# Seven block products in place of eight for the FFN input product of a decoder step

## The chip, the cores and the metric

The kernel runs on one core of a Trainium2 chip. Its engines are TensorE (PE, with its weight loads as PEld), VectorE (DVE), ScalarE (ACT), GpSimd (POOL) and SyncE (SP), each of which works through a queue of its own in order. The time is device microseconds for one execution, the median over runs; the profile is one execution more, with a time of its own.

## The reference: what is computed

One layer of a hybrid decoder (retention, gated MLP with spatial mixing, merge, FFN) over 512 prompt tokens and 8 sample tokens, so 520 columns in all, with width 1024. The part that matters here is the FFN:

```
D_FF = ((8 * D_MODEL // 3 + 255) // 256) * 256        # 2816
...
hn = rms_norm(h, norm_ffn_g)
f_gate, f_up = jnp.split(hn @ w_ffn_in, 2, axis=-1)
h = h + ((jax.nn.silu(f_gate) * f_up) @ w_ffn_down).astype(x.dtype)
...
y = rms_norm(h, norm_final_g)
```

All of it is float32. `w_ffn_in` is 1024 x 5632, `w_ffn_down` 2816 x 1024.

## The kernel before

Activations lie transposed: 128 features on the partitions, the 520 tokens along the free dimension, in two halves of 260 (`HT`). TensorE multiplies in a reduced form of float32 (fp32r), so each operand is split in two: `hi` is the value rounded to fp32r, `lo` is what is left. `split` makes `hi` on ACT and `lo` on DVE. A product of two operands is then three matmuls, hi x hi, hi x lo and lo x hi.

`weights` loads one tile of 128 x 1024 weights by SP (`wraw`, three buffers) and splits it into `whi` and `wlo` (two buffers each). `product` issues the matmuls of one 128 x 128 piece: three terms by two token halves, six matmuls of 128x260. A weight tile with eight such pieces is 48 matmuls into one PSUM tile of two banks (`acc_psum`, two buffers).

The last stages run in this order. `w_o` (tiles `ps_wo`): eight tiles of 48 matmuls; each result plus the residual goes to `hs`, and ACT and DVE make the scaled split `hg` of it. Then the FFN input: for each of 22 tiles of 128 hidden features one tile of the gate (`ps_fg`) and one of the up half (`ps_fu`); DVE multiplies both with `rstd`, ACT takes the silu, POOL multiplies gate and up (`fa`), and `split` makes `act`. Then the FFN output (`ps_fd`): eight tiles of 22 pieces, 132 matmuls each. The last of the eight is done in two token halves of 66 matmuls, so that the final norm of the first half (a sum over features by a matmul with ones, `ps_ss`, then four DVE and ACT operations for the root, then the scaling of all rows and the store) runs beside the matmuls of the second half.

The order on each engine comes from a scheduler that places instructions when the program is built; the pools of buffers bound it. `big` holds 26 pairs of 128 x 2 x 520, and the FFN keeps its `act` tiles there.

The names: `wraw`, `whi`, `wlo` are weights as loaded and split; `hg` and `act` are activations; `ps_...` are PSUM tiles; `fa`, `fb` are gate and up values.

Of the kernel before, what the change touches and what calls it, by code (L numbers as in the profile page):

```python
# [29 lines left out]
NBIG = 26  # L30
NFP = 4
# [10 lines left out]
def step_kernel(ctx: ExitStack, tc: tile.TileContext, io):  # L42
# [41 lines left out]
    def weights(src, n, cuts=(), keep=False):  # L84

        raw = wp.tile([P, 8 * P], F32, name="wraw", tag="wraw", bufs=3)
        if keep:
            hi, lo = flat(wide("khi", F32R)), flat(wide("klo", F32R))
        else:
            hi = wp.tile([P, 8 * P], F32R, name="whi", tag="whi")  # L90
            lo = wp.tile([P, 8 * P], F32R, name="wlo", tag="wlo")
# [448 lines left out]
    def gmlp(gp):  # L540
# [187 lines left out]
    a = None  # L728
    for i in range(NF):
        a, b = ttile("fa"), ttile("fb")  # L730
        pg = ev(ffn_tile(i, "ps_fg"))
        if i == 0:

            nc.scalar.copy(out=halves(a), in_=pg)
            pg = halves(a)
            pu = ev(ffn_tile(NF, "ps_fu"))
            nc.scalar.copy(out=halves(b), in_=pu)
            pu = halves(b)
            row_rstd(rstd, row_sums(sq), D)
            sq = const.tile([P, T], F32, name="sq")  # L740
        nc.vector.tensor_tensor(out=halves(a), in0=pg, in1=halves(rstd), op=ALU.mult)
        nc.scalar.activation(out=a, in_=a, func=AF.Silu)
        if i > 0:
            pu = ev(ffn_tile(NF + i, "ps_fu"))
        nc.vector.tensor_tensor(out=halves(b), in0=pu, in1=halves(rstd), op=ALU.mult)  # L745
        nc.gpsimd.tensor_tensor(out=a, in0=a, in1=b, op=ALU.mult)  # L746
        pr = fp.tile([P, 2, T], F32R, name=f"act{i}") if i < NFP else pair(f"act{i}")
        split(pr[:, 0, :], pr[:, 1, :], a)
        act.append(pr)

    def down_weights(i, keep=False):

        for k0 in range(0, NF, 8):
            n = min(8, NF - k0)
            yield weights(io["w_ffn_down"][i][:, k0 * P : (k0 + n) * P], n, keep=keep), k0, n

    def down(ps, blocks, fs=(0, 1)):
        for w, k0, n in blocks:
            for k in range(k0, k0 + n):
                product(ps, w, k - k0, act[k], k == 0, k == NF - 1, fs)  # L760

    rsqrt_table(a)

    hn = []
    for i in range(KT - 1):
        ps = acc_psum("ps_fd")
        down(ps, down_weights(i))
        hi = hs[:, i, :]
        nc.vector.tensor_tensor(out=halves(hi), in0=ev(ps), in1=halves(hi), op=ALU.add)
        add_square(sq, hi, i == 0)  # L770
        nc.scalar.activation(out=hi, in_=hi, func=AF.Copy, scale=gains[:, 2, i : i + 1])
        hn.append(hi)
# [102 lines left out]
```

## Time and profile before

| what | value |
|---|---|
| median of 3 runs | 1168.37 us (1165.16 to 1168.41) |
| the profiled execution's own time | 1165.98 us |
| its span, first to last instruction | 1164.2 us |
| instructions in the span | 21641 |
| mean granted TensorE clock | 0.990 |
| PE busy | 1142.0 us, 98% of the span |
| DVE busy | 668.8 us, 57% |
| ACT busy | 435.8 us, 37% |
| POOL busy | 209.8 us, 18% |

Busy time of PE counts overlapping matmuls once, and a pipelined matmul's record is longer than what it adds; what one matmul adds is read from a stretch of many. The time outside the span, 1165.98 less 1164.2, is 1.8 us.

### The profile page before, as it was taken

The numbers are of one execution on the slowest core, as the hardware profiler recorded it, in microseconds if no ns is written. First come the engines' busy times: TensorE is split into PE (matmuls) and PEld (weight loads), VectorE is DVE, ScalarE is ACT, GpSimd is POOL, SyncE is SP. The second block draws the span as 40 slices with busy tenths as digits, with TensorE's granted clock in tenths as the row PEclk, the third lists the DMA queues.
The fourth block names the chain that finished last, engine by engine and source line by source line (L and its number), as shares of the span: only waits on it lengthen the run. The fifth ranks groups of instructions, "written<-read, shape, count | busy, mean of one in ns | idle before, by whom it ended". The sixth has DMA issues, their size and how long they took to land.

```text
span 1164.2 us, 21641 instructions
## 1 busy us (share of the span) xinstructions
PE 1142.0 (98%) x9242; PEld 1125.6 (97%) x9242; DVE 668.8 (57%) x1040; ACT 435.8 (37%) x672; POOL 209.8 (18%) x175
## 2 busy tenths in 40 slices
PE   8999999999999999999999999999999999999995
PEld 7999999999999998999999999999999999999995
DVE  7788738885787589538434456445545454532233
ACT  4366345433653365323223432343222232322220
POOL 7213201420141013002111222211101010101101
PEclk9999999999999999999999999999999999999998
DMA  7267336633763284222222223422232222223222
GB/s 266 86 217 286 110 110 237 244 109 117 261 212 127 74 276 162 73 91 74 90 74 73 91 91 117 139 94 92 88 106 81 104 90 93 87 90 97 86 78 74
DMA packets 44928, 147.53 MB, mean 127 GB/s; under 512 B 5360, under 2 KB 7808, under 8 KB 44824
## 3 DMA queue, kind: packets, MB, share of 16 engines
q1 hardware_dynamic: 37152, 118.76, 30.2%
q0 software_dynamic: 7680, 27.38, 6.4%
q8 instruction: 73, 1.20, 0.4%
q14 instruction: 23, 0.19, 0.0%
HBM read 125.02 MB, written 21.10 MB: 126 GB/s over the span
## 4 chain that ended last, share of the span: by engine, by line
PE 84%; DVE 7%; DMA 3%; ACT 3%; issue 2%; POOL 0%; DVEq 0%; ACTq 0%; POOLq 0%; SPq 0%
PE ps_fg L105 11%; PE ps_fu L105 11%; PE ps_fd L105 10%; PE ps_ro L105 8%; PE ps_v L105 6%; PE ps_ar L105 4%; PE ps_gm L105 4%; PE ps_g L105 4%; PE ps_gu L105 4%; PE ps_wo L105 4%; PE ps_gv L105 4%; PE ps_ag L105 3%; PE k L105 3%; PE q L105 2%; PE ps_o L460 1%
## 5 line engine op out<-in xcount | busy, mean ns | idle before, releaser
L79 ACT CAST whi<-wraw 128x1024 fp32r<-128x1024 f32 (+2 forms) x180 | 184.8, 1027 | 484.9 <-issue 96.3
L82 DVE TENSOR_TENSOR wlo<-wraw,whi 128x1024 fp32r<-128x1024 f32 (+2 forms) x180 | 256.4, 1425 | 99.2 <-ACT whi L79 94.4
L105 PE MATMUL ps_fg<-hg,whi 128*128 128x260 f32 x704 | 112.5, 282 | 0.0
L105 PE MATMUL ps_fu<-hg,whi 128*128 128x260 f32 x704 | 112.5, 282 | 0.0
L105 PE MATMUL ps_fd<-act,whi 128*128 128x260 f32 x616 | 98.8, 282 | 0.0
L105 PEld LDWEIGHTS ps_fg<-hg,whi 128*128 128x128 f32 x704 | 96.2, 188 | 0.0
L105 PEld LDWEIGHTS ps_fu<-hg,whi 128*128 128x128 f32 x704 | 96.2, 188 | 0.0
L105 PEld LDWEIGHTS ps_fd<-act,whi 128*128 128x128 f32 x616 | 84.4, 188 | 0.0
L105 PE MATMUL ps_g<-xg,whi 128*128 128x260 f32 x512 | 82.7, 283 | 0.0
L105 PE MATMUL ps_ro<-gated,whi 128*128 128x260 f32 x512 | 82.6, 283 | 0.0
L105 PE MATMUL ps_v<-xg,whi 128*128 128x260 f32 x512 | 82.3, 282 | 0.0
L105 PEld LDWEIGHTS ps_ro<-gated,whi 128*128 128x128 f32 x512 | 70.6, 188 | 0.7 <-issue 0.2
L105 PE MATMUL ps_fu<-hg,wlo 128*128 128x260 f32 x352 | 70.8, 282 | 0.0
L105 PE MATMUL ps_fg<-hg,wlo 128*128 128x260 f32 x352 | 70.8, 282 | 0.0
L105 PEld LDWEIGHTS ps_v<-xg,whi 128*128 128x128 f32 x512 | 70.1, 188 | 0.0
L105 PEld LDWEIGHTS ps_g<-xg,whi 128*128 128x128 f32 x512 | 69.9, 188 | 0.0
L746 POOL TENSOR_TENSOR fa<-fa,fb 128x520 f32<-128x520 f32 x22 | 28.8, 1308 | 227.6 <-ACT whi L79 192.8
L442 ACT ACTIVATE kv<-qkb,vs 128x256 f32<-128x256 f32 x128 | 54.1, 498 | 26.9 <-DMA qkb<-qks 23.9
L105 PE MATMUL ps_fd<-act,wlo 128*128 128x260 f32 x308 | 61.8, 282 | 0.0
L745 DVE TENSOR_TENSOR fb<-ps_fu,rstd 128x520 f32<-128x520 f32 x21 | 14.7, 700 | 75.1 <-PE ps_fu L105 75.1
L163 POOL TENSOR_TENSOR sq<-sq,sqr 128x520 f32<-128x520 f32 x19 | 32.9, 1732 | 132.7 <-ACT sqr L161 128.4
L447 DVE SCALAR_TENSOR_TENSOR junk<-S,qkb 128x256 f32<-128x256 f32 x128 | 54.0, 422 | 2.3
(250 smaller groups left out, 2509.3 us busy)
## 6 DMA issues: line engine op xcount, KB each, us to landing
wraw<-in_w_in SPq DMA_DIRECT2D x78, 512.0 KB, 3.5
wraw<-in_w_ffn_in SPq DMA_DIRECT2D x44, 512.0 KB, 3.5
S<-in_st SPq DMA_DIRECT2D x32, 512.0 KB, 4.4
out_rss<-S POOLq DMA_DIRECT2D x32, 512.0 KB, 4.6
qkb<-qks POOLq DMA_DIRECT2D x16, 512.0 KB, 5.0
wraw<-in_w_ret_o SPq DMA_DIRECT2D x16, 512.0 KB, 3.5
wraw<-in_w_ffn_down SPq DMA_DIRECT2D x16, 512.0 KB, 3.5
wraw<-in_w_gm_o SPq DMA_DIRECT2D x8, 512.0 KB, 3.5
```

The lines of the kernel that those rows point to most:

```text
L79: nc.scalar.copy(out=hi, in_=src)
L82: (lo_eng or nc.vector).tensor_tensor(out=lo, in0=src, in1=hi.bitcast(F32), op=ALU.subtract)
L105: nc.tensor.matmul((ps[f] if isinstance(ps, list) else ps[:, f])[:, 0:HT], a, x[:, k, f * HT : (f + 1) * HT], start=first and n == 0, stop ...
L163: (add or nc.gpsimd).tensor_tensor(out=acc, in0=acc, in1=q, op=ALU.add)
L442: nc.scalar.activation(out=kv[:, j, :], in_=kb, func=AF.Copy, scale=vs[:, j, b : b + 1])
L447: nc.vector.scalar_tensor_tensor(out=junk, in0=S[:, j, :], scalar=1.0, in1=qb, op0=ALU.mult, op1=ALU.mult, accum_out=os_[:, j, b : b + 1],)
L460: nc.tensor.matmul(ps[:, s * P : NP], vtile(s, l)[:, j * P : (j + 1) * P], score(s, k), start=i == 0, stop=i == 11,)
L745: nc.vector.tensor_tensor(out=halves(b), in0=pu, in1=halves(rstd), op=ALU.mult)
L746: nc.gpsimd.tensor_tensor(out=a, in0=a, in1=b, op=ALU.mult)
```

## The change

The FFN input product is regrouped. A block is now two pieces of 128 hidden features (the gate and the up tile of the same number) by two halves of the 1024 input features, against the two token halves: a 2 x 2 by 2 x 2 product of blocks. In place of eight block products there are seven (Strassen's algorithm), each of four pieces by three terms by one half of tokens, 12 matmuls of 128x260 (`seven`, order a, b, s1, s2, s3, s4, d). They accumulate into three PSUM banks, and between products partial sums are copied out or added (`seen`).

The activations' sums are formed once, after `w_o` (`sum_acts`). The weights' sums are formed for each of 22 blocks (`sum_weights`): `s13` by two plain loads and an adding DMA issued by POOL, `s24` by two DVE additions, and the block `d` by a casting DMA into `wdh`, a negated copy on ACT into `wdl`, and an adding DMA into `wdl`. Three pairs of 128 x 1024 are then split as before.

Hidden features are handled in groups of 8, 8 and 6: up to ten blocks of the input product are run, then the output product over a group's pieces, added to `hs` (DVE multiplies with `rstd`, POOL adds); the last group takes the final norm. `rstd` is multiplied in before the silu by POOL, and the up half's factor after the output product. The pools are changed: `big` has 24, tables of the first stages lie in pools that are closed after the heads, and their room holds two more buffers each of `wraw`, `whi` and `wlo` (`wq`) and two of `wdh` and `wdl`.

```
-NBIG = 26
-NFP = 4
+NBIG = 24
+NACT = 10
...
+    wpools = {"wraw": [wp] * 3, "whi": [wp] * 2, "wlo": [wp] * 2}
...
+    first.close()
+    wq = ctx.enter_context(tc.tile_pool(name="wq", bufs=2))
+    for k in wpools:
+        wpools[k] = wpools[k] + [wq] * 2
...
+    ORDER = "a b s1 s2 s3 s4 d".split()
+    MEETS = dict(a=0, s1=1, b=2, d=6, s4=3, s3=4, s2=5)
...
+        s13 = block(wtile("wraw", F32))
+        for i in range(2):
+            nc.sync.dma_start(out=s13[:, i], in_=src[:, 0])
+        nc.gpsimd.dma_start(out=s13, in_=src[:, 1:3], accum_op=ALU.add)
+        ab = block(wtile("wraw", F32))
+        nc.sync.dma_start(out=ab, in_=src[:, 2:4])
+        dh = wq.tile([P, 4 * P], F32R, name="wdh")
+        dl = wq.tile([P, 4 * P], F32R, name="wdl")
+        nc.gpsimd.dma_start(out=dh, in_=src[:, 1])
+        nc.scalar.activation(out=dl, in_=dh.bitcast(F32), func=AF.Copy, scale=-1.0)
+        nc.gpsimd.dma_start(out=dl, in_=src[:, 1], accum_op=ALU.add)
+        s24 = block(wtile("wraw", F32))
+        nc.vector.tensor_tensor(out=s24[:, 0], in0=s13[:, 0], in1=ab[:, 0], op=ALU.add)
+        nc.vector.tensor_tensor(out=s24[:, 1], in0=s24[:, 0], in1=ab[:, 1], op=ALU.add)
+        w = {"d": (dh, dl)}
+        for names, t in (("a b", ab), ("s1 s3", s13), ("s2 s4", s24)):
+            w |= dict(zip(names.split(), both(t.rearrange("p a b -> p (a b)"))))
...
+            tt(out=x[:, 4], in0=x[:, 3], in1=x[:, 1], op=ALU.subtract)
+            tt(out=x[:, 1], in0=x[:, 0], in1=x[:, 1], op=ALU.subtract)
+            stt(out=x[:, 5], in0=x[:, 3], scalar=-1.0, in1=x[:, 1], op0=ALU.mult, op1=ALU.subtract)
+            stt(out=x[:, 6], in0=x[:, 5], scalar=-1.0, in1=x[:, 2], op0=ALU.mult, op1=ALU.subtract)
...
+            split(h, l, x[:, 0:4])
...
+        bank = [ps[:, 0, 0:HT], ps[:, 1, 0:HT], aux(f"{name}3")[:, 0:HT]]
+        into = dict(a=0, b=2, s1=1, s2=0, s3=0, s4=1, d=0)
...
+                for n, (ww, xx) in enumerate(((w[s][0], xh), (w[s][0], xl), (w[s][1], xh))):
+                    nc.tensor.matmul(
+                        bank[to], ww[:, sl], xx, start=to not in begun,
...
+            seen(s, bank)
...
-        pr = pair(f"hg{i}")
-        scaled_split(pr, hi, gains[:, 1, i : i + 1])
-        hg.append(pr)
...
+            if s == "a":
+                nc.scalar.copy(out=a[:, L], in_=bank[0])
+            elif s == "b":
+                nc.vector.tensor_tensor(out=a[:, L], in0=a[:, L], in1=bank[2], op=ALU.add)
+            elif s == "s1":
+                nc.scalar.activation(out=b[:, R], in_=bank[1], func=AF.Copy, scale=-1.0)
+            elif s == "s2":
+                nc.scalar.copy(out=a[:, R], in_=bank[0])
+            elif s == "s3":
+                nc.vector.tensor_tensor(out=b[:, R], in0=b[:, R], in1=bank[0], op=ALU.subtract)
+            elif s == "s4":
+                nc.vector.tensor_tensor(out=a[:, R], in0=a[:, R], in1=bank[1], op=ALU.add)
...
+                nc.gpsimd.tensor_tensor(out=a, in0=a, in1=rstd, op=ALU.mult)
+                nc.scalar.activation(out=a, in_=a, func=AF.Silu)
+                nc.gpsimd.tensor_tensor(out=b[:, R], in0=a[:, R], in1=b[:, R], op=ALU.mult)
+            else:
+                nc.vector.scalar_tensor_tensor(
+                    out=b[:, L], in0=bank[0], scalar=-1.0, in1=a[:, L], op0=ALU.mult, op1=ALU.mult
...
+            t = ttile("fd")
+            nc.vector.tensor_tensor(out=halves(t), in0=ev(ps), in1=halves(rstd), op=ALU.mult)
+            nc.gpsimd.tensor_tensor(out=hi, in0=hi, in1=t, op=ALU.add)
...
+    for n in (8, 8, 6):
+        for i in range(done, min(k0 + NACT, NF)):
+            ffn_in(i)
...
+        ffn_down(k0, n, k0 + n == NF)
...
-    blocks = list(down_weights(i, keep=True))
+    w = down_weights(i, k0, n)
```

How this moves instructions is shown at three places.

The first place is ACT in the middle of the FFN input stage. Before, two weight tiles of one feature number are cast (`whi`), with the silu (`fa<-fa`) and the cast of the result (`act`) between them:

```order
L742 ACTIVATE fa<-fa 128x520
L79 CAST whi<-wraw 128x1024
L79 CAST act_9373<-fa 128x520
L79 CAST whi<-wraw 128x1024
L742 ACTIVATE fa<-fa 128x520
```

In the change, some two thirds of a period of two blocks read so; `wdl<-wdh` is the negated copy that waits for the casting DMA, and L857, L861 and L863 take partial sums out of PSUM:

```order
L88 CAST whi<-wraw 128x1024 x2
L857 COPY fa<-ps_f 128x260
L747 ACTIVATE wdl<-wdh 128x512
L88 CAST whi<-wraw 128x1024
L861 ACTIVATE fb<-ps_f 128x260
L871 ACTIVATE fa<-fa 128x520
L863 COPY fa<-ps_f 128x260
L88 CAST act_9707<-fb 128x520
L747 ACTIVATE wdl<-wdh 128x512
L88 CAST whi<-wraw 128x1024
```

The negated copy stands in the queue ahead of a weight cast, and behind the silu and the cast of a result.

The second place is DVE from the last `hs` of the `w_o` stage to the last activation that the FFN input waits for. Before, that is the split of `hg`:

```order
L712 TENSOR_TENSOR hs<-ps_wo,xr 128x520
L82 TENSOR_TENSOR wlo<-wraw,whi 128x1024
L182 SCALAR_TENSOR_TENSOR hg_8871<-hs,gains,hg_8871 128x520
```

In the change it is `hxl`, the lo part of four blocks at once (`xsum` are the activations' sums, `hxm` their lo parts):

```order
L834 TENSOR_TENSOR hs<-ps_wo,xr 128x520
L91 TENSOR_TENSOR wlo<-wraw,whi 128x1024
L167 TENSOR_TENSOR sq<-sq,sqr 128x520
L765 TENSOR_TENSOR xsum<-xsum 128x260
L750 TENSOR_TENSOR wraw<-wraw 128x512
L766 TENSOR_TENSOR xsum<-xsum 128x260
L91 TENSOR_TENSOR sql<-sq,sqh 128x520
L751 TENSOR_TENSOR wraw<-wraw 128x512
L796 TENSOR_TENSOR hxm_8907<-xsum,hxm_8905 128x260
L767 SCALAR_TENSOR_TENSOR xsum<-xsum 128x260
L149 TENSOR_SCALAR rr_v<-ps_ss 128x260 x2
L91 TENSOR_TENSOR hxl_8920<-xsum,hxh_8919 128x1040
```

Three instructions have become twelve rows.

The third place is the end of PE's queue: the second token half of the last output tile and its sum over features. Before, the last rows of the second half's 66 matmuls are these:

```order
L105 MATMUL ps_fd_12611<-act_11515,khi 128x260 x2
L105 MATMUL ps_fd_12611<-act_11515,klo 128x260
L790 MATMUL ps_ss<-sq,ones_f 128x260
```

In the change the sums of the first half stand ahead of the whole second half, which is 18 matmuls (its first and last rows are shown apart):

```order
L928 MATMUL ps_ss<-sq,ones_f 128x260
L936 MATMUL ps_ss<-sq,ones_f 128x260
L928 MATMUL ps_ss<-sq,ones_f 128x260
L109 MATMUL ps_fd_13022<-act_11568,whi 128x260 x2
L109 MATMUL ps_fd_13022<-act_11568,wlo 128x260
```
```order
L109 MATMUL ps_fd_13022<-act_12667,whi 128x260 x2
L109 MATMUL ps_fd_13022<-act_12667,wlo 128x260
L936 MATMUL ps_ss<-sq,ones_f 128x260
```

What moved: 48 of the 66 matmuls of the second half now run in earlier groups.

## Rows read from the trace of the kernel before

**Rows 1.** The page, part 1: busy time, share, instructions.
```profile
PE 1142.0 (98%) x9242; PEld 1125.6 (97%) x9242; DVE 668.8 (57%) x1040; ACT 435.8 (37%) x672; POOL 209.8 (18%) x175
```

**Rows 2.** Chain that ended last, in time: start, us, what.
```profile
794.09 5.73 PE ps_fg L105 x48
799.82 5.73 PE ps_fu L105 x48
...
1023.15 118.58 PE ps_fd L105 x990
```

**Rows 3.** Busy time in the FFN input stage: stretch, engines, clock, DMA share, GB/s.
```profile
800.00:1000.00 200.00, 200.00 (x1679) 200.00 (x1678) 96.77 (x87) 57.23 (x70) 22.23 (x17) 1.00 0.27 93
```

**Rows 4.** The tile ps_fg: duration ns min/median/max.
```profile
L105 PE MATMUL ps_fg<-hg,whi x704: 277/282/287, 770.5 to 1016.9; 128*128 128x260 f32 x176
...
L105 PE MATMUL ps_fg<-hg,wlo x352: 278/282/287, 771.0 to 1017.1; 128*128 128x260 f32 x176
```

**Rows 5.** Groups by shape, 800 to 1000: count, busy us, mean ns, idle.
```profile
L82 DVE TENSOR_TENSOR wlo<-wraw,whi 128x1024 fp32r<-128x1024 f32 x35 | 62.1, 1773 | 6.0 <-ACT whi L79 3.5
...
L79 ACT CAST whi<-wraw 128x1024 fp32r<-128x1024 f32 x35 | 36.8, 1051 | 118.7 <-PE ps_fu L105 70.9 <-PE ps_fg L105 47.7
L746 POOL TENSOR_TENSOR fa<-fa,fb 128x520 f32<-128x520 f32 x17 | 22.2, 1307 | 172.5 <-ACT whi L79 162.4 <-issue 10.1
L741 DVE TENSOR_TENSOR fa<-ps_fg,rstd 128x520 f32<-128x520 f32 x18 | 12.6, 700 | 33.5 <-PE ps_fg L105 33.5
...
L82 DVE TENSOR_TENSOR act<-fa,act 128x520 fp32r<-128x520 f32 x17 | 11.7, 687 | 0.0
L742 ACT ACTIVATE fa<-fa 128x520 f32<-128x520 f32 x18 | 11.5, 640 | 0.0
L79 ACT CAST act<-fa 128x520 fp32r<-128x520 f32 x17 | 10.7, 629 | 22.7 <-POOL fa L746 22.7
```

**Rows 6.** The tile wlo, 800 to 1000: duration ns min/median/max.
```profile
L82 DVE TENSOR_TENSOR wlo<-wraw,whi x35: 1224/1227/2378, 800.7 to 995.4; 128x1024 fp32r<-128x1024 f32 x35
```

**Rows 7.** Timelines of DVE and POOL: shapes near the new ones.
```profile
277.71 0.69 DVE L82 TENSOR_TENSOR scl<-sct,sch 128x512 fp32r<-128x512 f32 x1 [1.15 <-PE ps_ro L105]
...
1151.52 0.41 DVE L787 TENSOR_TENSOR hs<-ps_fd,hs 128x260 f32<-128x260 f32 x1
...
767.17 1.80 POOL L163 TENSOR_TENSOR sq<-sq,sqr 128x520 f32<-128x520 f32 x1 [3.92 <-DVE wlo L82]
```

**Rows 8.** DVE's line L799 and POOL's: ns min/median/max.
```profile
L799 DVE TENSOR_TENSOR hs<-hs,r x9: 415/418/977, 1148.5 to 1158.5; 128x260 f32<-128x260 f32 x9
L799 POOL TENSOR_TENSOR hs<-hs,r x5: 732/931/1000, 1148.2 to 1156.4; 128x260 f32<-128x260 f32 x5
```

**Rows 9.** POOL's DMAs: one issue group; then KB each, us to landing.
```profile
L444 POOL DMA_DIRECT2D out_rss<-S x32 | 17.0, 533 | 186.8 <-DVE S L443 186.8
...
qkb<-qks POOLq DMA_DIRECT2D x16, 512.0 KB, 5.0
out_rsp<-sf POOLq DMA_DIRECT2D x4, 512.0 KB, 3.2
out_gmv<-gvs POOLq DMA_DIRECT2D x1, 32.0 KB, 2.1
```

**Rows 10.** The page, part 2: GB/s in 40 slices.
```profile
GB/s 266 86 217 286 110 110 237 244 109 117 261 212 127 74 276 162 73 91 74 90 74 73 91 91 117 139 94 92 88 106 81 104 90 93 87 90 97 86 78 74
```

**Rows 11.** Chain that ended last, from w_o to the FFN input: start, us, what.
```profile
770.69 5.25 PE ps_fg L105 x44
...
782.15 0.47 PE ps_ss L173 x4
782.63 5.74 PE ps_fg L105 x48
```

**Rows 12.** Chain that ended last, at the end: start, us, what.
```profile
1141.74 0.88 PE ps_ss L784 x4
...
1145.65 0.44 DVE rr_v L135
...
1151.59 0.35 DVE hs L787
...
1157.56 1.36 DVE hs L799 x4
```

**Rows 13.** Busy time in two early stretches: columns as in rows 3.
```profile
400.00:500.00 100.00, 98.00 (x759) 94.23 (x758) 70.62 (x145) 47.51 (x91) 16.10 (x18) 0.98 0.47 159
500.00:600.00 100.00, 98.78 (x797) 97.39 (x796) 54.06 (x95) 30.85 (x43) 17.23 (x9) 0.97 0.24 80
```

More of the change, by code (lines that the diff above doesn't have):

```diff
@@ L74, in ev, with wtile @@
         return ps[:, :, 0:HT]
+    def wtile(kind, dt=F32R):
+        pools = wpools[kind]
+        pool = pools[wturn[kind] % len(pools)]
+        wturn[kind] += 1
+        return pool.tile([P, 8 * P], dt, name=kind, tag=kind, bufs=pools.count(pool))
     def split(hi, lo, src, hi_eng=None, lo_eng=None):
@@ L82, in split, with weights @@
         (lo_eng or nc.vector).tensor_tensor(out=lo, in0=src, in1=hi.bitcast(F32), op=ALU.subtract)
[L84 to L91, printed above, removed]
+    def weights(src, n, cuts=()):
+        raw, hi, lo = wtile("wraw", F32), wtile("whi"), wtile("wlo")
         at = [0, *cuts, n]
@@ L194, in load @@
     def load(name, shape, src):
-        t = const.tile(shape, F32, name=name)
+        t = pa.tile(shape, F32, name=name)
         nc.sync.dma_start(out=t, in_=src)
@@ L726, in step_kernel, with ffn_in @@
+    hx = sum_acts(fill_h, "hx", KT // 2)
     rstd = const.tile([P, T], F32, name="rstd")
     act = []
-    a = None
-    for i in range(NF):
+    L, R = slice(0, HT), slice(HT, T)
+    def ffn_in(i):
         a, b = ttile("fa"), ttile("fb")
[L731 to L739, printed above, removed]
-            sq = const.tile([P, T], F32, name="sq")
[L741 to L772, printed above, removed]
+        def seen(s, bank):
+            if s == "a":
[10 more added lines that the diff above has]
+                nc.vector.tensor_tensor(out=a[:, R], in0=a[:, R], in1=bank[1], op=ALU.add)
+                if i == 0:
+                    row_rstd(rstd, row_sums(sq), D)
+                nc.gpsimd.tensor_tensor(out=a, in0=a, in1=rstd, op=ALU.mult)
+                nc.scalar.activation(out=a, in_=a, func=AF.Silu)
+                nc.gpsimd.tensor_tensor(out=b[:, R], in0=a[:, R], in1=b[:, R], op=ALU.mult)
+            else:
+                nc.vector.scalar_tensor_tensor(
+                    out=b[:, L], in0=bank[0], scalar=-1.0, in1=a[:, L], op0=ALU.mult, op1=ALU.mult
+                )
@@ new lines, in ffn_in, with down, down_weights, ffn_down @@
+        seven(sum_weights(io["w_ffn_in"][i].rearrange("p (s c) -> p s c", s=4)), hx, "ps_f", seen)
+        pr = pair(f"act{i}")
+        split(pr[:, 0, :], pr[:, 1, :], b)
+        act.append(pr)
+    def down(ps, w, k0, n, fs=(0, 1)):
+        for k in range(n):
+            product(ps, w, k, act[k0 + k], k == 0, k == n - 1, fs)
+    def down_weights(i, k0, n):
+        return weights(io["w_ffn_down"][i][:, k0 * P : (k0 + n) * P], n)
+    def ffn_down(k0, n, last=False):
+        for i in range(KT - last):
+            ps = acc_psum("ps_fd")
+            down(ps, down_weights(i, k0, n), k0, n)
+            hi = hs[:, i, :]
+            t = ttile("fd")
+            nc.vector.tensor_tensor(out=halves(t), in0=ev(ps), in1=halves(rstd), op=ALU.mult)
+            nc.gpsimd.tensor_tensor(out=hi, in0=hi, in1=t, op=ALU.add)
+            if last:
+                add_square(sq, hi, i == 0)
+                nc.scalar.activation(out=hi, in_=hi, func=AF.Copy, scale=gains[:, 2, i : i + 1])
+                hn.append(hi)
```

110 lines of the change are left out of this document (91 added, 19 removed).

## The prediction

> **What bounds the kernel now.** I read the busy times first, then the chain of waits, then the stretches by stage, then the groups by shape within the FFN input stage. PE is busy 98% of the span [rows 1], and the chain shows why that share means something here: through the FFN it consists of nothing but matmuls, tile after tile of 48 in 5.73 us, 118.58 us for the output product [rows 2]. One matmul therefore adds 5.73/48 = 0.1194 us, although its record reads 282 ns [rows 4]; the records overlap. Between 800 and 1000 PE has no gap, DVE is busy 96.8 of 200 us, ACT 57.2, POOL 22.2 [rows 3]. So this stage is bound by the number of matmuls, and half of DVE and most of ACT and POOL are free to be spent.
>
> **Part by part. What is removed.** The gate tiles take 704 + 352 = 1056 matmuls [rows 4], the up tiles as many: 2112, or 96 for each of 22 blocks. In the changed order I count 84 for each (seven products of 12). 22 x 12 x 0.1194 = **31.5 us less**. The output product keeps its matmul count, only regrouped.
>
> **DVE in a block.** Before, a block of 11.46 us holds two `wlo` (1.227 at the median [rows 6]), two evictions (0.700) and the split of `act` (0.687 [rows 5]): 4.54 us. After, a block must fit in 84 x 0.1194 = 10.03 us. It holds three `wlo`, 3.68; two additions of 128x512 by 0.69, 1.38; four evictions of 128x260 by 0.41 [rows 7], 1.64; the `act` split, 0.69: 7.4 us. To this comes what POOL takes from DVE. The mean `wlo` is 1773 ns against a median of 1227: 35 x 0.546 = 19.1 us lost, beside 22.2 us of POOL's multiplications [rows 5, 6], or 0.86 us for each us of POOL. POOL's new work in a block is 1.31 for 128x520 [rows 5] and 0.73 for 128x260 [rows 8], 2.04 us, so DVE loses 1.75 and stands at **9.2 of 10.03 us**. It fits, with little to spare.
>
> The Trainium skill (SBUF — State Buffer, "Who interferes with whom") says that a DVE instruction with two SBUF inputs contends with a POOL instruction that reads SBUF, one blocking the other outright. That agrees with the long `wlo` here, and it speaks against this change, which adds instructions of just that kind to both engines; by the rule evictions from PSUM stay out of it, as do descriptor writes beside such additions (inferred there), and the block would stand near the 9.2 us.
>
> **ACT in a block.** Three weight casts of 1.05, silu 0.64, cast of `act` 0.63 [rows 5], the negated copy about 0.55 and three evictions about 0.4 each (estimates from the cast by size): 6.2 us. Not full, but its order matters. The negated copy waits for the casting DMA into `wdh`, which POOL issues right after multiplying `fa` with `rstd`. Between that issue and ACT's turn lie the silu 0.64, POOL's 0.73, the eviction of d 0.41 and the cast of `act` 0.63, so about 2.4 us of landing are hidden. The trace has no casting load of 256 KB. POOL's DMAs landed in 2.1 (32 KB), 3.2 and 5.0 us (512 KB) [rows 9]; I take 3.2, the plain one of them, and keep 2.1 and 5.0 as bounds. ACT is then held 0.8 us. Queued behind is a weight cast. In one block of two it is the a b pair, which PE wants 12 matmuls (1.43 us) after its buffer is freed: 1.43 less the cast's 1.05 leaves a cushion of 0.4, so 0.4 us reaches PE; in the other block PE needs what stands behind much later. That is 0.2 us a block. The skill's DMA: Bandwidth & Descriptors ("Anatomy of one DMA — SWDGE (gpsimd) path") fits 2.0 us plus bytes over 436 GB/s, an estimate of 2.6 us here; by that the cushion would take it all. For DVE at 92% I add 0.2 us a block, between 0 and the 1.75 of the rival below, nearer the low end since 9.2 is under 10.03. Together 22 x 0.4 = **8.8 us more**.
>
> **DMAs.** A block moves 2 MB into SBUF instead of 1 MB: 205 GB/s over 10 us, below the 286 that a slice of this kernel moved [rows 10]. The adding DMA of `s13` is asked for more than a block ahead (five `wraw` for three in a block), so even 10 us for load and addition together would be hidden by matmuls; without that cover a block would wait for the excess. POOL's issues are 0.53 us each [rows 9], three a block; with 2.04 of multiplying, POOL is at 3.6 of 10.
>
> **From `w_o` into the FFN.** Before, PE waits for nothing: 770.69 to 782.63 is 96 matmuls (11.46) and the 0.47 of the sums [rows 11]. After, DVE has twelve rows from the last `hs` to the `hxl` that the matmuls need: 0.70 + 1.23 + 0.69 + 0.41 + 0.69 + 0.41 + 0.69 + 0.69 + 0.41 + 0.41 + two of about 0.4 + 1.24 = 8.4 us. PE has 48 matmuls to go on with, 5.7 us. The wait is 2.7; ACT's squares and casts come between, so I take **3.5**, bounds 2.7 and 6.
>
> **Into the output product, three times.** Its second tile needs the PSUM buffer of the block just ended, so an eviction with its semaphores stands bare: about 0.7 us each (0.41 and the gaps), **2.1 us**. Back into the input product the weights have been prepared beside output tiles, where DVE has 1.9 us of work in 5.7; nothing. The additional evictions of 8, 8 and 8 tiles lie beside the next tile's 48 or 36 matmuls.
>
> **The end.** The chain from the first half's end at 1141.74 runs without the second half's matmuls: root and scaling of the first half, then at 1151.59 the eviction of the second, then the same again [rows 12]. So the 66 matmuls of the second half cost nothing today. After, only 18 lie there; the other 48 run earlier, on the path: 48 x 0.1194 = 5.7 us, plus one more DVE operation, the product with `rstd`. The start of the first half's root is as late as before: the sum of squares of tile seven (eviction 0.70, POOL 1.31, square 0.64, POOL 1.31) ends some 2.4 us after the first half's matmuls, and the trace has 3.9 us from there to `rr_v`. **6.0 us more.**
>
> **Early stages.** The order up to the retention's end is nearly the same; around 450 to 510 more weight buffers change it. PE lacks 2.0 and 1.2 us in these stretches [rows 13]; a gain is at most these 3, a loss (ACT's first negated copies stand there) about as much. I take 0.
>
> **Sum.** -31.5 + 8.8 + 3.5 + 2.1 + 6.0 = -11.1, on the profiled execution's 1165.98: **1155 us**. Its own time is 2.4 below the median of the runs and within their spread, so I leave it at that. About 0.3% (3.5 us) is what a measurement of this kernel can tell from no change.
>
> **Rivals.** *DVE becomes the bound, slower.* If POOL's operations are stretched as the 1.80 us one [rows 7], pass on in full, and the DMA issues (3 x 0.53) do so too, a block is 7.4 + 1.80 + 1.0 + 1.6 = 11.8 us of DVE, 1.75 over: 38.5 us in place of 8.8, so 1185. It decides from 0.9 us a block (19.9 us are left of the gain before waits, over 22). For it: 92% already. Against: before, PE lost nothing to such stretching.
>
> *ACT is held by the casting DMA, slower.* With a landing of 5.0 ACT waits 2.6, less 0.4 of cushion, in every second block: 1.1 a block, with the 0.2 for DVE 28.6 us: 1146.1 + 28.6 = 1175. For it: 5.0 stands for all sixteen large loads that POOL issues. Against: that one is twice the size and reads scratch just written.
>
> *Everything is hidden, faster still.* No waits in the blocks and the 3 us of the early stages gained: 1146.1 - 3 = 1143. Against: the cushions are thin.
>
> **How the numbers follow.** Forecast (waits of 0 to 0.7 a block, 1146 to 1161) 0.58; all hidden 0.12; ACT held 0.14; DVE bound 0.12; 0.04 for the rest, spread evenly. A milder form of the two waits falls near no change, so of their 0.26 I give 0.08 to "same" and 0.02 to "faster". Faster 0.73, same 0.09, slower 0.18. The range that leaves out 2 in 10 goes from 1142 to 1175; the forecast's own is 1146 to 1161.
>
> **What would show it.** 1848 matmuls in the FFN input in place of 2112; a period of two blocks of 20.1 to 21.5 us; DVE near 9 us in each block; ACT's idle time before the negated copy put down to the `wdh` DMA and under 1 us; a gap of 3 to 4 us ahead of the first `hxl`; PE idle for some 2.4 us ahead of the first half's sums at the end, and 15 to 17 us from the last output matmul to the end of the span. The prediction is wrong if a period of two blocks comes near 22 us, if `wdh` lands in 4 us or more, or if the additions of `s13` land too late for DVE.

## The result and the profile after

The changed kernel takes **1203.82 us** (median of 4 runs, 1202.59 to 1210.7) against 1168.39 us beside it: a ratio of 1.0315, 95% interval 1.0275 to 1.0354. It is 35.4 us slower; I had forecast 1155 and a range of 1142 to 1175. The profiled execution is the slowest of the four (1210.7 us, span 1209.0).

The busy times of the page and, for the stretch from the last matmul of `w_o` (778.8) to the last of the input product (1156.2), the busy time of PE, PEld, DVE, ACT and POOL, the granted clock, the DMA share and GB/s:

```profile
PE 1137.1 (94%) x8978; PEld 1113.8 (92%) x8978; DVE 761.1 (63%) x1192; ACT 500.2 (41%) x790; POOL 313.0 (26%) x286
```
```profile
778.80:1156.20 377.40, 338.21 (x2651) 332.13 (x2649) 218.31 (x264) 151.45 (x222) 121.39 (x118) 0.96 0.57 140
```

PE has fewer matmuls than before, and yet it is busy for a smaller share of a longer span [rows 1]. In this stage, where it had no gap at all [rows 3], it now idles for 39.2 of 377.4 us, and the granted clock has fallen from 1.00 to 0.96. DVE is busy 58% of the time. So nothing is full: not PE, not DVE, not the DMA engines (0.57). That picture asks who waits for whom.

The sum of this stage, which serves for every kernel below: it holds 1848 matmuls of the input product (1848 x 0.1194 = 220.7 us) and sixteen tiles of the output product (16 x 5.73 = 91.7 us). What is over, 377.4 - 312.4 = **65.0 us, I call lost**. The forecast had some 14 of that (8.8 in blocks, 3.5 in the transition, 2.1 at the entries). Idle time is 39.2 of the 65.0; of the rest, in which PE counts as busy, up to some 15 go with the clock (below).

The chains of waits in this stage, first PE's own, then those behind them (who waited for what: us in all, times, longest):

```profile
PE ps_f L817 <- DVE fb L874: 19.1, 9, 3.6
PE ps_f L817 <- ACT fa L857: 8.0, 3, 4.1
PE ps_f L817 <- DVE fa L867: 7.9, 4, 3.5
...
POOL wraw L741 <- DMA wraw<-in_w_ffn_in: 76.4, 12, 18.9
POOL wdl L748 <- ACT wdl L747: 54.2, 16, 5.9
POOL fa L870 <- DVE fa L867: 49.9, 13, 8.4
...
DVE wraw L750 <- DMA wraw<-in_w_ffn_in: 38.0, 15, 5.4
...
ACT wdl L747 <- DMA wdh<-in_w_ffn_in: 30.9, 13, 4.6
```

PE waits above all for three evictions: L874 (the last of a block), L867 and L857. PE wants the PSUM bank that they empty. An eviction takes 0.4 us, so the question is why it comes late. Three blocks in time, on DVE the addition L750 and the eviction L874 that follows it, on PE the next matmul with its idle time:

```profile
805.29 0.69 DVE L750 TENSOR_TENSOR wraw<-wraw 128x512 f32<-128x512 f32 x1 [2.87 <-DMA wraw<-in_w_ffn_in]
805.90 0.42 DVE L874 SCALAR_TENSOR_TENSOR fb<-ps_f,fa 128x260 f32<-128x260 f32 x1
806.38 0.39 PE L817 MATMUL ps_f<-hxh,whi 128*128 128x260 f32 x1 [2.60 <-DVE fb L874]
...
816.36 0.69 DVE L750 TENSOR_TENSOR wraw<-wraw 128x512 f32<-128x512 f32 x1 [4.17 <-DMA wraw<-in_w_ffn_in]
816.96 0.42 DVE L874 SCALAR_TENSOR_TENSOR fb<-ps_f,fa 128x260 f32<-128x260 f32 x1
817.44 0.39 PE L817 MATMUL ps_f<-hxh,whi 128*128 128x260 f32 x1 [1.97 <-DVE fb L874]
...
831.48 1.89 DVE L750 TENSOR_TENSOR wraw<-wraw 128x512 f32<-128x512 f32 x1 [2.83 <-DMA wraw<-in_w_ffn_in]
833.51 0.43 DVE L874 SCALAR_TENSOR_TENSOR fb<-ps_f,fa 128x260 f32<-128x260 f32 x1
834.00 0.39 PE L817 MATMUL ps_f<-hxh,whi 128*128 128x260 f32 x1 [3.25 <-DVE fb L874]
```

This is read from top to bottom in each group of three: DVE stands idle for weights that come by DMA; the eviction, queued behind, leaves as soon as the addition has; PE has waited 2.60, 1.97 and 3.25 us for it. The order of DVE's instructions in the program says whose weights these are (row numbers of that list come first; those behind an underscore belong to tiles: `fb_8930` is block 0, and the sums `wraw_8942`, `9088`, `9215` and `9342` are those of blocks 0 to 3):

```
751 L750 TENSOR_TENSOR wraw_9342<-wraw_9331,wraw_9335 128x512
752 L874 SCALAR_TENSOR_TENSOR fb_8930<-ps_f_8957,fa_8929 128x260
```

The addition for block 3 stands ahead of the last eviction of block 0, and the same pair follows in the next four blocks. The Trainium skill (PSUM — Partial Sum Buffer, "Engine vs sequencer instructions") says that the queues of ACT, DVE and POOL are strictly first in, first out; the trace agrees, with 5.4 us as the longest time for which DVE stood before an addition (at 881.14; PE lost 3.31 there).

The landings between 785 and 1020, after and then before (KB each, median us from issue to landing):

```profile
wraw<-in_w_ffn_in SPq DMA_DIRECT2D x30, 256.0 KB, 4.4
wraw<-in_w_ffn_in POOLq DMA_DIRECT2D x14, 512.0 KB, 6.4
wraw<-in_w_ffn_in SPq DMA_DIRECT2D x14, 512.0 KB, 5.0
...
wdh<-in_w_ffn_in POOLq DMA_DIRECT2D x14, 256.0 KB, 4.6
wdl<-in_w_ffn_in POOLq DMA_DIRECT2D x13, 256.0 KB, 6.7
```
```profile
wraw<-in_w_ffn_in SPq DMA_DIRECT2D x37, 512.0 KB, 3.5
```

The adding DMA of `s13` follows its plain loads, so `s13` takes 4.4 + 6.4 us and what it waits in POOL's queue; a plain load of 512 KB now needs 5.0 us in place of 3.5; and `wdh` lands in 4.6, where I had taken 3.2.

The clock costs something besides. Three stretches of 4 us, columns as above:

```profile
816.00:820.00 4.00, 2.56 (x14) 2.56 (x15) 2.33 (x4) 0.77 (x2) 0.00 (x0) 0.77 0.89 252
832.00:836.00 4.00, 2.00 (x14) 2.00 (x15) 3.86 (x5) 2.12 (x3) 2.05 (x3) 0.91 0.96 177
836.00:840.00 4.00, 3.48 (x20) 3.18 (x20) 2.36 (x4) 2.79 (x4) 1.79 (x2) 0.67 0.54 164
```

After two of PE's idle spells (1.97 us and 3.25 us, above) part of the next stretch runs at the lower of the two levels (1.2 in place of 2.4 GHz): from 836 to 840 PE is busy 3.48 us and gets 20 matmuls done, 0.174 us each in place of 0.119. Over the whole stage the granted clock was 0.96, by which this takes at most some 15 of the 65.0 us (0.04 x 377.4, an estimate).

### The profile page after: what moved, and what is told of

It reads as the page before. It is cut to its first block, busy times and chain, and to the rows that moved or that the text cites. A ratio compares the mean times of both kernels' runs of the same rounds, so it can differ in the third digit from the quotient of the medians.

```text
span 1209.0 us, 21757 instructions
## 1 busy us (share of the span) xinstructions
PE 1137.1 (94%) x8978; PEld 1113.8 (92%) x8978; DVE 761.1 (63%) x1192; ACT 500.2 (41%) x790; POOL 313.0 (26%) x286
## 4 chain that ended last, share of the span: by engine, by line
PE 63%; DMA 14%; DVE 11%; issue 4%; ACT 4%; POOL 1%; DVEq 0%; SPq 0%; POOLq 0%; ACTq 0%
PE ps_f L817 10%; PE ps_fd L109 10%; PE ps_ro L109 8%; DMA wraw<-in_w_ffn_in 7%; PE ps_v L109 5%; PE ps_gu L109 4%; PE ps_ar L109 4%; PE ps_gm L109 4%; PE ps_ag L109 3%; DVE wlo L91 3%; PE k L109 3%; PE ps_gv L109 3%; PE ps_wo L109 3%; DMA wdh<-in_w_ffn_in 3%; DMA S<-in_st 2%
## 5 line engine op out<-in xcount | busy, mean ns | idle before, releaser
L88 ACT CAST whi<-wraw 128x1024 fp32r<-128x1024 f32 (+3 forms) x205 | 210.2, 1027 | 350.7 <-issue 75.8
L91 DVE TENSOR_TENSOR wlo<-wraw,whi 128x1024 fp32r<-128x1024 f32 (+3 forms) x205 | 293.3, 1433 | 75.1 <-ACT whi L88 68.2
L817 PE MATMUL ps_f<-hxh,whi 128*128 128x260 f32 x352 | 104.4, 299 | 28.4 <-DVE fb L874 19.1
L817 PE MATMUL ps_f<-hxl,whi 128*128 128x260 f32 x352 | 103.2, 294 | 1.8 <-DVE hxl L91 1.8
L817 PE MATMUL ps_f<-hxh,wlo 128*128 128x260 f32 x352 | 102.0, 294 | 0.0
L817 PEld LDWEIGHTS ps_f<-hxh,whi 128*128 128x128 f32 x352 | 69.4, 198 | 32.1 <-DVE fb L874 21.0
L817 PEld LDWEIGHTS ps_f<-hxl,whi 128*128 128x128 f32 x352 | 70.3, 200 | 2.0 <-DVE hxl L91 2.0
L817 PEld LDWEIGHTS ps_f<-hxh,wlo 128*128 128x128 f32 x352 | 69.8, 200 | 0.4 <-DVE wlo L91 0.4
L817 PE MATMUL ps_f<-hxm,whi 128*128 128x260 f32 x352 | 68.2, 291 | 0.2 <-ACT fb L861 0.2
L817 PEld LDWEIGHTS ps_f<-hxm,whi 128*128 128x128 f32 x352 | 56.9, 197 | 0.4 <-ACT fb L861 0.4
```

The source lines that it names most:

```text
L817: nc.tensor.matmul(bank[to], ww[:, sl], xx, start=to not in begun, stop=k == len(acts) - 1 and n == 2, skip_group_check=True,)
```

## The experiments

The kernels ran in four series, each beside the kernel before, whose median was 1166.73 (with the kernels e), 1165.83 (f), 1166.51 (g) and 1166.55 us (h). The table gives the median, its distance from the kernel before of the same series, the interval of the ratio, and the us lost in the FFN input stage of its profile by the sum above.

| kernel | what differs | us | from before | ratio, 95% | lost |
|---|---|---|---|---|---|
| changed kernel | | 1203.82 | +35.4 | 1.0275 to 1.0354 | 65.0 |
| e1_plain_s13 | no adding DMA for s13 | 1180.31 | +13.6 | 1.0095 to 1.0146 | 42.8 |
| e2_split_d | d by load and split | 1182.71 | +16.0 | 1.0119 to 1.0177 | 40.7 |
| e3_no_pool_dma | both | 1158.68 | -8.1 | 0.9917 to 0.9968 | 20.2 |
| e4_eight_regrouped | eight products | 1172.90 | +6.2 | 1.0036 to 1.0073 | |
| f1_pin_dve | e2, additions tied | 1170.56 | +4.7 | 1.0025 to 1.0058 | 30.6 |
| f2_pin_dve_pool | f1, adding DMA tied | 1171.46 | +5.6 | 1.0036 to 1.0078 | 31.5 |
| f3_pin_all | changed kernel, order tied | 1190.49 | +24.7 | 1.0199 to 1.0245 | 49.6 |
| f4_dve_sums | all sums on DVE | 1186.08 | +20.3 | 1.0151 to 1.0194 | 47.3 |
| g1_products_dve | f1, POOL's products to DVE | 1166.11 | -0.4 | 0.9986 to 1.0020 | 27.5 |
| g2_six_raw | f1, a sixth raw buffer | 1165.08 | -1.4 | 0.9969 to 1.0002 | 22.6 |
| g3_neg_ready | changed kernel, ACT doesn't wait for wdh | 1184.47 | +18.0 | 1.0126 to 1.0187 | 53.2 |
| g4_both | g1 and g2 | 1160.46 | -6.1 | 0.9925 to 0.9962 | 19.5 |
| h1_tied_neg_ready | f3, ACT doesn't wait for wdh | 1183.08 | +16.5 | 1.0088 to 1.0188 | 42.3 |
| h2_tied_products_dve | f3, POOL's products to DVE | 1176.57 | +10.0 | 1.0058 to 1.0124 | 36.6 |

### Which part costs the time

**e1_plain_s13**

```
-        for i in range(2):
-            nc.sync.dma_start(out=s13[:, i], in_=src[:, 0])
-        nc.gpsimd.dma_start(out=s13, in_=src[:, 1:3], accum_op=ALU.add)
+        nc.sync.dma_start(out=s13, in_=src[:, 1:3])
```

> s13 comes by one plain load of the second and third block of columns on SP's queue; the two loads of the first block and the adding DMA are left out, so s1, s3, s2 and s4 are not the sums they should be, while every operation of DVE, ACT and PE stays. Theory A (the sums' latency: plain load 4 us, then the adding DMA with 6 to 8 us whose issue waits in POOL's queue, then DVE, which has the additions ahead of splits that PE waits for): of the 66 us that PE loses in the 22 blocks some 40 to 45 go, 1160 us, between 1152 and 1172. Rival B (ACT is held by the casting DMA into wdh and POOL by the negated copy): little changes, 1190 to 1204. Rival C (DVE is the bound): 1195 or more, since DVE's work is the same.

21.8 us came back (35.4 - 13.6), half of what theory A wanted; 1180.3 lies in none of the three ranges. What remains has the other signature:

```profile
POOL wdl L746 <- ACT wdl L745: 89.6, 20, 6.7
...
ACT wdl L745 <- DMA wdh<-in_w_ffn_in: 33.5, 14, 5.1
```

**e2_split_d**

```
-        nc.gpsimd.dma_start(out=dh, in_=src[:, 1])
-        nc.scalar.activation(out=dl, in_=dh.bitcast(F32), func=AF.Copy, scale=-1.0)
-        nc.gpsimd.dma_start(out=dl, in_=src[:, 1], accum_op=ALU.add)
+        dr = fp.tile([P, 4 * P], F32, name="wdr", bufs=2)
+        nc.sync.dma_start(out=dr, in_=src[:, 1])
+        split(dh, dl, dr)
```

The excerpt leaves out that in this kernel, and in e3, f1, f2, g1, g2 and g4, the activations' sums lie in two of the big tiles instead of a tile of their own, to make room.

> d comes by a plain load on SP and the usual split (cast on ACT, difference on DVE, 0.69 us more of DVE in a block); POOL issues the adding DMA of s13 alone. To make room, the sums of the activations lie in two of the big tiles instead of a tile of their own. Theory A (latency of s13's load and addition): the cycle stays, only the early loss of 8 us and a part of ACT's holds go: 1185 to 1198. Rival B (wdh and wdl hold ACT and POOL): the stall goes, 1150 to 1170. Rival C (DVE is the bound): slower than the changed kernel, by up to 15 us (22 x 0.69), 1205 to 1220.

19.4 us came back, although DVE has more to do: C is out, and 1182.7 lies between what A and B had. DVE's wait for the `s13` weights and PE's for the evictions stay:

```profile
POOL wraw L741 <- DMA wraw<-in_w_ffn_in: 65.7, 10, 18.7
...
DVE wraw L750 <- DMA wraw<-in_w_ffn_in: 33.7, 17, 5.6
...
PE ps_f L821 <- DVE fb L878: 13.4, 9, 3.4
```

**e3_no_pool_dma**: both edits.

> Both edits: s13 by one plain load (its sums left out), d by plain load and split; no DMA is left on POOL's queue in this stage. Theories A and B: PE finds its weights, 1145 to 1160. Rival C (DVE is the bound): 1185 or more, with DVE over 95 per cent busy in the blocks. If it stays above 1175 with DVE under 80 per cent, neither the adding DMAs nor DVE's amount of work was the cause, and the order of the instructions or the number of buffers is.

8.1 us faster than before. The two parts add up: `s13`'s adding DMA is worth 21.8 (changed kernel to e1) and 24.1 (e2 to e3), `d`'s two DMAs 19.4 and 21.7. Together they are 43.5 us (what the moved sums of the activations do is in the price of `d`'s), and what is left comes to within 3 us of the gain that I had forecast (-11.1).

**e4_eight_regrouped**: the changed kernel's frame around `product(ps, w, kt, hg[kt], ...)` for the gate and the up tile, as in the kernel before.

> The changed kernel's pools, its output product in groups of 8, 8 and 6 and its end, but the input product by eight products with ordinary splits: the rest of the change by itself. Theories A and B: by my terms 1168 + 2.1 for the three entries + 6.0 at the end, and up to 3 either way for the early stages: 1173 to 1180. Rival D (the rest of the change costs the time: pools, regrouping, end): 1190 or more.

6.2 us: entries, end and pools together cost what the prediction had put down for them (8.1), a little less. Rival D is out.

### Why the sums come late

**f1_pin_dve**, on top of e2; `behind` adds an edge to the scheduler's input, so that an instruction stands behind another in its engine's queue, without a wait:

```
+        with behind("d", n - 2):
             nc.vector.tensor_tensor(out=s24[:, 0], in0=s13[:, 0], in1=ab[:, 0], op=ALU.add)
             nc.vector.tensor_tensor(out=s24[:, 1], in0=s24[:, 0], in1=ab[:, 1], op=ALU.add)
```

> On top of e2_split_d (1182.7 us, its s13 still made by the adding DMA): the two additions of s24 for block n are tied on DVE behind the last eviction of block n-2, so that they no longer stand ahead of evictions of earlier blocks; the output stays that of the reference. Theory A, now narrower (the s13 sums come late only because DVE, which works in order, was given the additions of a block up to three ahead, and then waits for their DMA while PE's PSUM banks and splits wait behind): 1160 to 1170. Rival E (too few raw buffers, so that the load and the addition are too late in any order): within 5 us of 1183, or slower. Rival F (POOL is what is held: the adding DMA waits in its queue for the plain loads, and the product with rstd behind it): 1176 to 1183, and the gain comes with f2.

11.3 us (16.0 - 4.7) from the tie: nothing was taken away, and the adding DMA lands no sooner (6.6 us against 6.7 in e2, both between 785 and 1020). The same place as above in time:

```profile
816.91 0.43 DVE L884 SCALAR_TENSOR_TENSOR fb<-ps_f,fa 128x260 f32<-128x260 f32 x1
817.26 0.75 DVE L756 TENSOR_TENSOR wraw<-wraw 128x512 f32<-128x512 f32 x1
```

The eviction is now ahead of the addition. DVE's wait for the `s13` weights and PE's for this eviction, above for e2, are now:

```profile
PE ps_f L827 <- DVE fb L884: 2.4, 2, 2.1
...
DVE wraw L756 <- DMA wraw<-in_w_ffn_in: 8.0, 3, 4.6
```

But 12.8 us to e3 remained, which theory A did not expect (1170.6 is half a us over its range).

**f2_pin_dve_pool**: f1, and `with behind("fb", n - 3):` around the adding DMA.

> f1 and besides the adding DMA of s13 for block n tied on POOL behind the product of block n-3. Theory A: a further 2 to 5 us over f1 at most, 1156 to 1168. Rival E: within 5 us of 1183, or slower. Rival F: 1158 to 1168 where f1 stayed above 1176.

Within 1 us of f1, and in none of the three ranges, although POOL's wait for the plain loads fell from 26.6 us in 7 waits (f1) to 7.7 in 5. So rival F, as I had put it, is out: that wait was not what the time hung on.

**g1_products_dve** takes POOL's two products away from f1, **g2_six_raw** gives a sixth raw buffer; **g4_both** is both.

```
-                nc.gpsimd.tensor_tensor(out=a, in0=a, in1=rstd, op=ALU.mult)
+                nc.vector.tensor_tensor(out=a, in0=a, in1=rstd, op=ALU.mult)
...
-                nc.gpsimd.tensor_tensor(out=b[:, R], in0=a[:, R], in1=b[:, R], op=ALU.mult)
+                nc.vector.tensor_tensor(out=b[:, R], in0=a[:, R], in1=b[:, R], op=ALU.mult)
```
```
+    wpools["wraw"] = wpools["wraw"] + [fp]
...
-        dr = fp.tile([P, 4 * P], F32, name="wdr", bufs=2)
+        dr = fp.tile([P, 4 * P], F32, name="wdr", bufs=1)
```

> On top of f1_pin_dve (1170.6): the products with rstd and with the up half move from POOL to DVE (about 1.1 us of DVE in a block for 2.04 of POOL), so that POOL's queue holds the adding DMAs of s13 alone in the blocks. Rival F (in f1 the adding DMA waits in POOL's queue for the plain loads and holds the product behind it): 1158 to 1165. Rival E (what is left is the time of load and addition, whatever stands behind them): 1167 to 1174. Rival C (DVE near its limit): slower than f1, 1172 to 1180.

> On top of f1_pin_dve (1170.6): a sixth buffer for the raw weights (one of two buffers of d's raw block given up for it), so that the loads of s13 can be asked for earlier. Rival E (the load and the addition, one after the other, find their buffer too late): 1158 to 1166. Rival F (POOL's queue) and theory A (order alone): 1167 to 1174.

> g1 and g2 together, the output that of the reference. If both E and F hold, 1155 to 1163, under the kernel before; if one alone holds, as the better of g1 and g2; C: 1170 to 1180.

g1 gained 5.1 us over f1 (it stands between the ranges of F and E), g2 6.1 and both 10.8. The buffers (E) hold about half of what the order on DVE had left, and the products on POOL the other half. For these I had named the queue (F); after f2 it is rather the products themselves (that with `rstd` took 1.735 us on POOL in f1, mean of 7 between 800 and 880, and 0.70 on DVE in g1) and what they take from DVE (below). Which of the two was not tried. g4, whose `s13` is still made by the adding DMA, stands 2.0 us from e3, where it is not (e3 with g4's two edits was not run). So the adding DMA, with its traffic and its landing of 6.9 us (median between 785 and 1020), need not cost what it costs in the changed kernel. g4 is faster than the kernel before by 6.1 us (ratio 0.9944, 0.9925 to 0.9962), and 41.5 us faster than the changed kernel by their distances from the kernel before. Its chain of waits, in time, through four blocks (left out: between `wraw` and `ps_f` two splits, an addition and an eviction on DVE):

```profile
817.01 0.68 DVE wraw L757
...
819.90 17.57 PE ps_f L828 x144
...
837.84 0.68 DVE wraw L757
...
840.72 17.49 PE ps_f L828 x144
...
858.58 0.68 DVE wraw L757
```

Two blocks take 20.83 and 20.74 us, and no DMA is on the chain of this stretch.

**f4_dve_sums**: two plain loads of 512 KB, four additions and `d`'s split on DVE.

```
+        split(dh, dl, s14[:, 1])
+        add(out=s32[:, 0], in0=s14[:, 0], in1=ab[:, 0], op=ALU.add)
+        add(out=s14[:, 0], in0=s14[:, 0], in1=s14[:, 1], op=ALU.add)
+        add(out=s32[:, 1], in0=s14[:, 0], in1=ab[:, 0], op=ALU.add)
+        add(out=s14[:, 1], in0=s32[:, 1], in1=ab[:, 1], op=ALU.add)
```

> No adding DMA and no DMA on POOL's queue: the four blocks of columns come by two plain loads of 512 KB, DVE makes all four sums and the split of d; the output stays that of the reference. DVE's work in a block grows by 2.07 us over the changed kernel, to 9.5 by my count and 11.2 with what POOL takes from it, against PE's 10.03. Theory A and C together (a DVE over its limit costs the excess): 1141 + 22 x 1.2 and some waits, 1165 to 1180. If what POOL takes does not add up: 1152 to 1163. If the adding DMAs were not the matter: 1190 or more.

Slower than theory A and C allowed. Between 785 and 870 DVE is busy 64.5 of 85 us, so it is not full as my count of 11.2 in 10.03 had it; PE waits for it all the same, briefly and often:

```profile
PE ps_f L817 <- DVE wlo L91: 11.4, 18, 0.9
PE ps_f L817 <- DVE fa L867: 7.4, 9, 1.5
```

These 18.8 us are a part of the 47.3 lost; the rest I did not settle. So doing without the adding DMA is no remedy by itself.

### What d's DMAs cost

**g3_neg_ready**, on the changed kernel:

```
-        nc.scalar.activation(out=dl, in_=dh.bitcast(F32), func=AF.Copy, scale=-1.0)
+        nc.scalar.activation(
+            out=dl.rearrange("p (a b) -> p a b", a=4), in_=ones_f[:, None, :].to_broadcast([P, 4, P]),
+            func=AF.Copy, scale=-1.0,
+        )
```

> The changed kernel with one edit: the negated copy on ACT reads a constant that is always there in place of wdh, so that ACT never waits for the casting DMA; both DMAs of d, POOL's order and all else stay, and d's low part is wrong. Theory B, narrow (ACT, which works in order, is held until wdh has landed, 32.6 us of waiting in all): 15 to 21 us of the 21 that e2 gave, 1183 to 1189. Rival G (POOL is what is held: wdh's issue waits for PE, that of the adding DMA for ACT, and s13's adding DMA stands behind): 1193 to 1204. Rival H (the traffic of the two additional DMAs slows the others): 1198 to 1206.

17.4 us came back of the 19.4 that e2 gave: in the order as it is, ACT's wait is what `d`'s DMAs cost, and neither the traffic nor POOL's issues as such. A prompt copy also ends POOL's wait for it (54.2 us in the changed kernel, above), so this does not tell what stood behind ACT from what stood behind POOL.

**f3_pin_all**: the changed kernel with `behind("d", n - 2)` for the additions, `behind("fb", n - 3)` for the adding DMA and `behind("s2", n - 1)` for the negated copy.

> The changed kernel itself, with wdh and wdl by the casting and the adding DMA as they are, and only the order tied: additions of s24 behind the last eviction of block n-2 (DVE), adding DMA of s13 behind the product of block n-3 (POOL), negated copy of wdh behind the s2 eviction of block n-1 (ACT). Theory A with B in its narrower form (each engine's order, not the amount of work, the landing or the buffers): 1158 to 1175 in place of 1203.8. Rival E: 1190 to 1210.

10.7 us, no more than f1 had from the additions alone: the two further ties gave nothing on balance. Theory A with B missed, and 1190.5 is the near end of rival E's range. The trace shows where waits now stand: ACT's weight casts wait for raw weights, which they do nowhere in this stage of the changed kernel, and ahead of evictions that PE waits for (us, times, longest; then ACT's queue in time):

```profile
PE ps_f L825 <- ACT fb L869: 10.8, 3, 5.3
...
ACT whi L88 <- DMA wraw<-in_w_ffn_in: 23.6, 9, 6.3
ACT wdl L754 <- DMA wdh<-in_w_ffn_in: 20.4, 15, 4.0
```
```profile
851.28 1.99 ACT L88 CAST whi<-wraw 128x1024 fp32r<-128x1024 f32 x2 [3.81 <-DMA wraw<-in_w_ffn_in]
853.88 0.63 ACT L754 ACTIVATE wdl<-wdh 128x512 fp32r<-128x512 f32 x1 [0.61 <-DMA wdh<-in_w_ffn_in]
854.41 0.37 ACT L869 ACTIVATE fb<-ps_f 128x260 f32<-128x260 f32 x1
```

PE stood 3.52 us for this eviction. **h1_tied_neg_ready** (f3 with g3's edit) and **h2_tied_products_dve** (f3 with g1's) ask what is ACT's wait for `wdh` in it, and what is POOL's queue.

> f3_pin_all (1190.5) with the edit of g3_neg_ready: the negated copy reads a constant in place of wdh (d's low part is wrong), the order tied as in f3. Theory B (ACT's wait for wdh is what d costs in f3 too): 1168 to 1176, where f1 stood with d by plain load. Rival G (POOL, whose issue of wdl stands ahead of the product with rstd): 1178 to 1186, since a prompt copy frees POOL only in part. Rival H (traffic of d's two DMAs): 1185 to 1192.

> f3_pin_all (1190.5) with both products on DVE, so that nothing that PE needs soon stands behind the DMA issues on POOL; wdh, wdl and ACT's order stay, and the output is that of the reference. Rival G: 1166 to 1176. Theory B: 1184 to 1192, since ACT waits for wdh as before. Both in part: about 1180. Rival H: 1186 to 1194.

8.2 us from h1 (whose runs spread from 1177 to 1186), 14.7 from h2, in which the tie of the adding DMA has no effect, since the product that it names is on DVE. h1 lies in rival G's range and h2 half a us over it: POOL's queue is the larger part. What ACT's wait for `wdh` costs by itself is not shown, since the prompt copy of h1 shortened POOL's wait for it too (57.0 to 33.0 us), while ACT's casts waited longer for raw weights (38.9 us in place of 23.6). h2 gives more, 9.6 of it beyond the 5.1 that the same edit gave f1, and f3's waits show what stood behind POOL (us, times, longest):

```profile
POOL wdl L755 <- ACT wdl L754: 57.0, 13, 6.6
...
POOL wdl L755 <- ACT fb L869: 16.3, 2, 8.5
```

The issue of `wdl` waits for ACT, and the product with `rstd`, which leads to the next eviction, waits behind it. That wait was there before (54.2 us in the changed kernel); the ties had left it. With 36.6 us lost, h2 is still 17 us behind g4, which has also the sixth buffer and `d` by load and split; these two were not taken apart on this side.

## Why the prediction was wrong

**The step that failed** is the one under "DMAs": "The adding DMA of `s13` is asked for more than a block ahead [...], so even 10 us for load and addition together would be hidden by matmuls". The landing was sized well enough (4.4 + 6.4 = 10.8 us). It *is* asked for far ahead, up to three blocks. But I compared that with when PE needs the weights, and not with where the first instruction stands that waits for them. That is DVE's addition, which the scheduler had put as far ahead as the request, before the evictions of the current block. I had asked of `wdh` who is queued behind the waiting instruction, and not of `s13`. The forecast had 0 for it; it cost 21.8 to 24.1 us: 11.3 by DVE's order (f1); of the rest g4 got back all but 2.0, with a sixth buffer and with faster products. These prices hold what the clock took after PE's idle spells, for which the forecast had no term at all. Two of the signs that the prediction had named for being wrong came: the additions of `s13` landed too late for DVE, and `wdh` took more than 4 us.

**The term that was mis-sized** is ACT's wait for `wdh`, 0.2 us a block. The mechanism was right and named as a rival (1175, with a landing of 5.0 us). `wdh` landed in 4.6 us rather than 3.2, and ACT waited 30.9 us in 13 waits, 2.4 each, where I expected under 1. I had 4.4 us for it in 22 blocks; `d`'s DMAs cost 19.4 to 21.7. With 4.6 put in for 3.2, my own working gives (4.6 - 2.4 - 0.4) / 2 = 0.9 us a block, 19.8 in all; that it comes so close is in part luck: ACT waited 13 times and not 11, and the cushion was not measured. I had taken the low one of two far bounds since the source and the size of the 5.0 row differed; the busier DMA engines (0.57 against 0.27 [rows 3]) were not part of the argument. The Trainium skill's fit for this path (DMA: Bandwidth & Descriptors, "Anatomy of one DMA — SWDGE (gpsimd) path"), an estimate of 2.6 us, was further off still; the measurement decides.

**What held.** The matmuls: 1848. DVE as the bound: no, 58% (the rival at 0.12); between 785 and 870 it worked 53.4 us beside 530 matmuls, 8.5 us for the 84 of a block, where I had 9.2. The regrouping with the end: 6.2 where I had 8.1; PE's idle time ahead of the first half's sums was 2.20 us (I had 2.4), and from the last output matmul (it starts at 1192.1) to the end of the span it is 16.9 us (15 to 17). The transition: PE was idle for 0.17, 0.70 and 1.82 us, 2.7 in all, the low bound (3.5 taken). The period of two blocks: 20.8 us in g4, as forecast (20.1 to 21.5), but only once the queues were freed. That POOL lengthens DVE's work also held, but at a lower price than my 0.86: with its products on DVE (g1) the mean `wlo` between 800 and 880 falls from 1373 to 1222 ns, the two groups being

```profile
L91 DVE TENSOR_TENSOR wlo<-wraw,whi 128x1024 fp32r<-128x1024 f32 x21 | 28.8, 1373 | 12.6 <-ACT whi L88 12.5
```
```profile
L91 DVE TENSOR_TENSOR wlo<-wraw,whi 128x1024 fp32r<-128x1024 f32 x23 | 28.1, 1222 | 8.0 <-ACT whi L88 7.9
```

of f1 and of g1. This is what the Trainium skill (SBUF — State Buffer, "Who interferes with whom") says of two SBUF inputs beside a reading POOL. With the first addition and `d`'s split, which shorten too (895 to 684 and 860 to 687 ns, seven each), f1's DVE lost 5.9 us beside 18.4 us of POOL's products, 0.32 for each. It did not decide the changed kernel's time; what part it has in g1's 5.1 us was not tried.

**The sum, as measured:** -31.5 for the matmuls, +6.2 for regrouping and end (e4), +43.5 for the two kinds of DMA (e3), and the remaining 17.2 for the transition and what else is lost in the blocks, where I had 12.3: +35.4.

**What stays open.** In the profiled execution the FFN input begins 8.1 us later than before (778.8 against 770.7); the other kernels begin it between 769.8 and 773.8, also f3 (771.6), which loads its first `wdh` at the same early place. So most of that probably belongs to this execution, the slowest of four, 6.9 us above their median; the forecast of 0 within 3 fits the others. A tied order makes the scheduler place everything else anew, so f1's and f3's gains include what moved with it.

## What to carry to other kernels

A transfer that is asked for early is hidden only if the first instruction that waits for it stands late: look up where that instruction stands in its engine's queue, and name what is behind it. Where a scheduler has set the order by its own idea of landing times, compare that idea with the landings in the trace; here tying two additions behind an eviction was worth 11 us without changing any work. And a tie that frees one in-order queue helps only as far as nothing urgent stands behind waits in the others: in f3 evictions stood behind ACT's casts and products behind POOL's issues.

## What the runs showed of the hardware

- Landings grow with the adding DMAs about: a plain load of 512 KB takes 5.0 us in the changed kernel, 3.5 before and 3.6 in e3; the DMA engines are busy 0.57 at 140 GB/s, and were 0.27 at 93 GB/s [rows 3]. So a byte occupied them 1.4 times as long.
- An adding DMA of 512 KB landed in 6.4 us, one of 256 KB in 6.7 in the same stretch.
- After some of PE's idle spells of 2 to 3 us the granted clock was 0.67 to 0.91 over 4 us, after others 1.00 (804 to 812). In g4, where they are gone, it is 1.00 between 785 and 870.
- Where nothing waits PE keeps its pace in the new blocks: between 842 and 858 g4 has 136 matmuls in 16.00 us of PE's busy time, the kernel before 137.
